# Prompt attention by pairs of heads from an earlier place, value products of two chunks side by side, and one pool of normed rows

## The chip, the cores and the metric

The kernel runs on one core of one Trainium2 chip. The time is device microseconds of one execution, and the kernel before takes 842.46 us (median of 3 runs, 838.32 to 845.08).

## What is computed

One layer of a hybrid decoder in float32, for a prompt of 512 rows and for 8 sequences of 4 new rows each (32 sample rows), which read 4096 past rows each from a paged cache. Cut to its core:

```
z = rms_norm(x, norm_mix) @ w_in                     # 1024 -> 2560 columns
q, k = rms_norm per head and half (4 heads x 2 x 64); v = z[1024:1536] (4 x 128)
u = gelu(z[1536:2048]); gv = rms_norm(gelu(z[2048:2560]))
p = softmax(mask(q k^T / 8))                         # per head and half, causal
att = (p[half 0] - lam * p[half 1]) @ v              # sample rows: over cache_k, cache_v and the new rows
mix = u * (tril(w_spatial) @ gv + b)                 # in chunks of 128 rows
h = x + [rms_norm(att) * 0.8 ; mix] @ w_out
y = h + relu(rms_norm(h) @ w_up)^2 @ w_down
```

It also returns the normed keys, the values and gv of the new rows.

## The kernel before

**Three streams share the engines.** TensorE (PE in the profile) runs the dense layers of the prompt: the input projection (`in_proj`), the output projection (`out_proj`) and eight groups of the feed-forward layer (`ffn`). Weights come in pieces of 512 KB on the SP queue and are split into two parts of reduced precision, `wh` (ScalarE, ACT) and `wl` (VectorE, DVE); the activations likewise into `Thi` and `Tlo`, and each product is three matmuls (`d<-wh,Thi`, `d<-wl,Thi`, `d<-wh,Tlo`; in `ffn` the weights are the stationary side).

**The input projection** goes through ten pieces of 256 columns in the order q0 q1 k0 k1 v0 v1 g0 g1 u0 u1 (`pi` 0 to 9), each in two halves of two row tiles (`tp`), each of these in two halves of the contraction: eight steps a piece, each ending in a `yield`. A step's follow-up work is put off by `later` and released by `flush`. Norms of q and k, and of attention rows, have a power on GpSimd (POOL, `rsqrt`).

**The prompt's attention** is a generator, `attention()`: 16 units (row tile i, head h) in the order of i. A unit is `attn_a` (scores `d<-r,r`, mask, maxima, exponentials, the two halves combined), one unit later `attn_b` (transposes `d<-idt,t`, copied out by ACT), two units later `attn_c` (product with v, `d<-r,t`). It advances once per step from step 11 of 20 on (`ATT0`, the second half of v1), two calls a unit, 36 calls in all. At that step everything put off is released at once and the pool of normed rows (`zn`) is closed and opened anew with 3 buffers in place of 8 (`local_pool(3)`), which makes room for attention's 6 tiles `t`.

**The samples' attention over the cache** is a list of small steps, `micro`: 64 chunks, each of 1 MB of keys and 1 MB of values, gathered by GpSimd's indirect DMA (`gK` into `kraw`, 2 buffers; `gV` into `v`, 3 buffers). DVE transposes a key chunk (`k_tr`, `kt<-kraw`), PE takes the scores of two chunks (`scores`, `S<-kt,qz`, 16 matmuls on 32 columns of the array each), and `LAG` = 11 chunk steps later the product with the values (`av`, `O<-v,PT`, 4 matmuls on 32 columns). `gV(n + 3)` is issued behind `av(n)` and waits for it, since it refills that chunk's buffer; `gK(n + 2)` behind `k_tr(n)`. `ptr` copies the transposed probabilities `PT` with 16 copies on ACT. With every `yield` the driver hands the step's cost to `pump`, which takes as many small steps as that cost pays for; so the cost that `attention()` yields moves the cache stream forward as well. A chunk step costs 6.1 units (TAU times 1.0), 0.6 of that before chunk 11 and 0.4 of it behind chunk 64, when no keys are left.

Each engine works through its own queue in order; within a window of 28 instructions on PE and DVE a scheduler decides that order when the kernel is built.

Of the kernel before, what the change touches and what calls it, by code (L numbers as in the profile page):

```python
# [19 lines left out]
NCH = 64  # L20
# [11 lines left out]
PLX = 2  # L32
WINDOW = 28
P_AT = 10
ATT0 = 11
ATTW = 2.4
D0 = 0.6
D1 = 0.4
# [24 lines left out]
def kernel(  # L63
# [76 lines left out]
    def st_():  # L140
        return sm.tile([128, 24], F32, tag="s", name="s")
# [46 lines left out]
    cst = const.tile([128, 13], F32, name="cst")  # L188
    rst = cst[:, 8:13]
    mhalf = const.tile([128, 24], F32, name="mhalf")  # L190
    rst8 = const.tile([128, 4], F32, name="rst8")
    ssb = [const.tile([128, 24], F32, name=f"ssb{i}") for i in range(2)]
    neglam = const.tile([128, 1], F32, name="neglam")
# [14 lines left out]
    ml = smp.tile([64, 32], F32, name="ml")  # L208

    WL = []  # L210
    for c0 in (0, 256, 512, 768, 1024, 1280, 2048, 2304, 1536, 1792):
        for hf in range(2):
            WL.append((wi[:, 4 * hf:4 * hf + 4, c0:c0 + 256], True))

# [446 lines left out]
    for n in range(NCH + LAG + 2):  # L661
        a, c = [], []
        if 1 <= n <= VB:
            a.append((gV, (n - 1,)))
        if n >= 2 and n % 2 == 0 and n <= NCH:
            a.append((scores, (n // 2 - 1,)))
            if n % 8 == 0:
                a.append((sm1, (n // 8 - 1,)))
        m = n - LAG
        if 0 <= m < NCH:  # L670
            a.append((av, (m,)))
            if m % 8 == 7:
                a.append((fin1, (m // 8,)))
        if m > 0 and m % 8 == 0:
            (a if m == NCH else c).append((fin2, (m // 8 - 1,)))
        for k, part, at, slot in ((0, 0, P_AT, a), (0, 1, P_AT, a), (1, 0, P_AT + 1, c), (1, 1, P_AT + 2, c)):
            if n >= at and (n - at) % 8 == 0 and (n - at) // 8 < 8:
                slot.append((ptr, ((n - at) // 8, k, part)))
        if 2 <= n < NCH:
            (a if n % 2 else c).append((k_tr, (n,)))  # L680
        if n >= 9 and (n - 1) % 8 == 0 and n - 1 <= NCH:
            a.append((sm2, (n // 8 - 1,)))
        d = D0 if n < LAG else D1 if n >= NCH else 1.0
        micro.append((d / 2, a))
        micro.append((d / 2, c))
# [134 lines left out]
    def in_proj(gm, F, gsrc, junk):  # L820
# [36 lines left out]
        att = attention()  # L857
        nt = new_tokens()
        for pi in range(10):
            kind, p = "qkvgu"[pi // 2], pi % 2  # L860
            if pi == 4:
                aux["vs"] = vgs
            if pi == 6:
                R3 = big.tile([128, 4 * T], F32, tag="r3", name="mix")
                R.append(R3)
                mix.append(R3[:, 0:2048].rearrange("p (n c) -> p n c", n=4))
                aux["gvs"] = vgs
            ss = ssb[pi % 2]
            items = []
            if kind == "q":  # L870
                A_, B_ = held[p]
            else:
                A_, B_ = w_get(), w_get()
            for tp in range(2):
                pss = {}
                if 2 * pi + tp == ATT0:
                    for _ in range(4):
                        flush()
                    local_pool(3)
                for half, w in ((0, A_), (1, B_)):  # L880
                    for t in (2 * tp, 2 * tp + 1):
                        cost = next(att, 0.0) if 2 * pi + tp >= ATT0 else 0.0
                        if half == 0:
                            pss[t] = dt_()[:, 0:256]
                        optB(pss[t], t, *w, half)
                        if t == 3 and (half == 0 or pi != 1):
                            w_conv()
                        if t % 2 == 1:
                            flush()
                        if half == 1:  # L890
                            post(kind, p, t, pss[t], 128, ss, items)
                            if pi == 4 and t == 0:
                                params()
                            if pi == 4 and t == 3:
                                params2()
                            if pi == 9 and t > 0:
                                cat_tile(t - 1)
                            if t == 3 and items:
                                finish_piece(kind, p, ss, items)
                            if pi == 0 and t == 1:  # L900
                                pinned(False)
                        elif pi == 5:
                            next(nt, None)
                        if pi == 0:
                            if t == 1 and half == 0:
                                x_stat(1, xt[1:4], 128, junk, G)
                                x_tile(3)
                            if t == 1 and half == 1:
                                masks(F, gsrc)
                            if t == 3 and half == 0:  # L910
                                gcols(gsrc)
                        if pi == 1 and t == 0 and half == 1:
                            load_params()
                        yield 1.3 + cost
                    if tp == 0 and kind != "q":
                        if half == 0:
                            sps = dt_()[0:64, 0:256]
                        packed(*w, [(4 * half + b, b) for b in range(4)], sps, half == 0, half == 1)
                        if half == 1:
                            post(kind, p, 4, combine(sps)[0:32], 32, ss, items)  # L920
                        yield 0.9
# [79 lines left out]

    def attn_c(i, h):
        at = aux.pop(("at", i, h))
        if h == 0:
            aux["oss"] = st_()
        ss = aux["oss"]
        o = dt_()[:, 0:128]
        for s in range(i + 1):
            mm(o, at[:, 128 * s:128 * s + 128], vN[:, s, 128 * h:128 * h + 128], s == 0, s == i)
        cat = qT[:, :, 128 * i:128 * i + 128]  # L1010
        a = aux.pop(("l", i, h))
        A.activation(out=cat[:, h, :], in_=o, func=ACTF.Copy, scale=a[:, 4:5])
        A.activation(out=o, in_=o, func=ACTF.Square, scale=a[:, 4:5], accum_out=ss[:, h:h + 1])
        if h == 3:
            rsqrt(ss[:, 0:4], EPS, 1.0 / 128.0)

            def go():
                for j in range(4):
                    V.scalar_tensor_tensor(out=cat[:, j, :], in0=cat[:, j, :], scalar=ss[:, j:j + 1], in1=sg,
                                           op0=ALU.mult, op1=ALU.mult)  # L1020
            later(go)
# [9 lines left out]
            split(ps.rearrange("p (k t) -> p k t", k=4), k0, i)  # L1031

    def attention():
        units = [(i, h) for i in range(4) for h in range(4)]
        n = len(units)
        for s in range(n + 2):
            cost = 0.0
# [8 lines left out]
            if 0 <= s - 2 < n:  # L1046
                attn_c(*units[s - 2])
                cost += 0.21 * (units[s - 2][0] + 1)
            yield ATTW * cost

    def out_proj(att):
        acc.extend(R[2 + m // 4][:, (m % 4) * T:(m % 4) * T + T] for m in range(8))
# [351 lines left out]
```

## Time and profile before

| | |
|---|---|
| runs | 842.46 us median (838.32 to 845.08) |
| the profiled execution | 842.67 us, of which the span of its instructions is 841.0 us |
| PE busy | 812.3 us (97% of the span) |
| DVE, ACT, POOL busy | 547.7, 357.9, 187.0 us |
| moved by DMA | 219.06 MB, mean 260 GB/s |

The stages in the span: 0 to about 42 us start and the samples' q; to about 300 us the input projection, with the prompt's attention (scores `d<-r,r`) from 130.1 to 260.9 us; to about 356 us the output projection; then the feed-forward groups. The cache stream runs from 42 to 582 us. A busy PE is not one at its peak, because ends of matmuls are modelled; what a piece of work costs PE is read from the start of one instruction to the start of the next.

### The profile page before, as it was taken

The page shows a single profiled execution, that of the slowest core. Times are in us where ns is not written, and L with a number is a line of the kernel's source. Part 1 is how long each engine was busy: PE and PEld are TensorE (multiplying, and loading weights), DVE is VectorE, ACT ScalarE, POOL GpSimd, SP SyncE. Part 2 cuts the span into 40 slices and gives each one's busy share as a digit, 9 for nine tenths or more (in the row PEclk, how much of TensorE's full clock was granted, in tenths as well). Part 3 has the DMA queues.
Part 4 walks back from the last instruction along what each step waited for, and adds up shares of the span by engine and source line. Part 5 has one row for each costly group of instructions (what it writes and reads, how often), then busy time and mean ns, then how long its engine had stood idle before and what let it go on. Part 6 is the DMA issues. An engine that isn't in the chain of part 4 may idle for free.

```text
span 841.0 us, 15425 instructions
## 1 busy us (share of the span) xinstructions
PE 812.3 (97%) x6210; PEld 630.6 (75%) x6210; DVE 547.7 (65%) x957; ACT 357.9 (43%) x888; POOL 187.0 (22%) x196
## 2 busy tenths in 40 slices
PE   5899999999899999999999999999999999999997
PEld 5788788676566788876666766655776898998997
DVE  5978766899888954787767576633844535444354
ACT  4543734776564652735144144163332431331231
POOL 4453532243432321212222232120100000000000
PEclk8899999999999999999999999999999999999999
DMA  8496799788788889877989797786398177577302
GB/s 316 156 376 227 264 356 317 298 317 328 279 312 322 296 307 334 291 244 281 321 316 344 294 346 275 281 294 230 116 317 267 61 237 245 177 234 232 101 14 94
DMA packets 101796, 219.06 MB, mean 260 GB/s; under 512 B 6088, under 2 KB 83996, under 8 KB 85340
## 3 DMA queue, kind: packets, MB, share of 16 engines
q0 software_dynamic: 18432, 134.23, 42.7%
q1 hardware_dynamic: 83292, 83.84, 30.5%
q8 instruction: 49, 0.80, 0.4%
q14 instruction: 23, 0.19, 0.1%
HBM read 213.53 MB, written 4.52 MB: 259 GB/s over the span
## 4 chain that ended last, share of the span: by engine, by line
PE 77%; DVE 8%; ACT 7%; DMA 5%; issue 2%; POOL 1%; SPq 0%; DVEq 0%; POOLq 0%; ACTq 0%
PE d L52 66%; PE O L52 6%; PE S L52 5%; DVE kt L52 3%; ACT PT L52 3%; DMA kraw<-in_cache_k_dram,idxK 2%; DMA raw<-in_w_in_dram 2%; DVE wl L52 1%; ACT wh L52 1%; DMA sg<-in_subln_gain_dram 1%; ACT z L52 1%; DVE s L52 1%; ACT t L52 1%; DVE zn L52 1%; ACT P L52 0%
## 5 line engine op out<-in xcount | busy, mean ns | idle before, releaser
L52 ACT CAST wh<-raw 128x1024 fp32r<-128x1024 f32 x90 | 94.1, 1047 | 189.2 <-PE d L52 175.4
L52 PE MATMUL d<-a,wh 128*128 128x272 f32 (+1 forms) x704 | 168.2, 342 | 0.4 <-DVE a L52 0.4
L52 DVE STREAM_TRANSPOSE kt<-kraw 128x2048 f32<-128x2048 f32 x64 | 146.8, 2300 | 13.5 <-PE S L52 7.1
L52 DVE TENSOR_TENSOR wl<-raw,wh 128x1024 fp32r<-128x1024 f32 x90 | 109.3, 1218 | 54.6 <-ACT wh L52 54.2
L52 PEld LDWEIGHTS d<-a,wh 128*128 128x128 f32 x704 | 112.8, 188 | 29.4 <-issue 7.1
L52 POOL DMA_INDIRECT v<-in_cache_v_dram,idxK x64 | 72.9, 1139 | 269.8 <-PE O L52 252.2
L52 PE MATMUL d<-wh,Thi 128*128 128x256 f32 x432 | 127.6, 296 | 0.6 <-ACT d L52 0.5
L52 PE MATMUL d<-wl,Thi 128*128 128x256 f32 x432 | 122.4, 283 | 0.0
L52 PE MATMUL d<-wh,Tlo 128*128 128x256 f32 x432 | 122.1, 283 | 0.2 <-DVE Tlo L52 0.2
L52 PE MATMUL d<-Thi,wh 128*128 128x272 f32 (+2 forms) x368 | 109.8, 339 | 0.0
L52 PE MATMUL d<-Tlo,wh 128*128 128x272 f32 (+2 forms) x368 | 106.7, 330 | 1.9 <-DVE Tlo L52 1.9
L52 PE MATMUL d<-Thi,wl 128*128 128x272 f32 (+2 forms) x368 | 106.8, 330 | 0.0
L52 PE MATMUL d<-a,wl 128*128 128x272 f32 (+1 forms) x352 | 102.7, 336 | 0.0
L52 PEld LDWEIGHTS d<-wh,Thi 128*128 128x128 f32 x432 | 81.6, 189 | 17.1 <-issue 11.5
L52 POOL DMA_INDIRECT kraw<-in_cache_k_dram,idxK x64 | 69.1, 1080 | 104.5 <-DVE kt L52 59.8
L52 PEld LDWEIGHTS d<-wh,Tlo 128*128 128x128 f32 x432 | 81.6, 189 | 0.9 <-issue 0.4
L52 PEld LDWEIGHTS d<-Thi,wh 128*128 128x128 f32 x368 | 63.7, 189 | 24.5 <-issue 15.0
L52 PEld LDWEIGHTS d<-wl,Thi 128*128 128x128 f32 x432 | 81.4, 188 | 0.0
L52 PE MATMUL O<-v,PT 128*32 128x512 f32 x512 | 73.4, 607 | 1.2 <-ACT PT L52 1.2
L52 ACT COPY PT<-d 32x128 f32<-32x128 f32 x256 | 65.6, 256 | 14.4 <-DVE d L52 11.0
L52 PEld LDWEIGHTS d<-Tlo,wh 128*128 128x128 f32 x368 | 63.9, 189 | 8.5 <-DVE Tlo L52 2.2
L52 PEld LDWEIGHTS d<-Thi,wl 128*128 128x128 f32 x368 | 63.7, 189 | 6.1
(265 smaller groups left out, 1069.3 us busy)
## 6 DMA issues: line engine op xcount, KB each, us to landing
raw<-in_w_up_dram SPq DMA_DIRECT2D x32, 512.0 KB, 5.3
raw<-in_w_down_dram SPq DMA_DIRECT2D x32, 512.0 KB, 3.9
plain<-in_w_up_dram SPq DMA_DIRECT2D x20, 512.0 KB, 4.3
plain<-in_w_down_dram SPq DMA_DIRECT2D x20, 512.0 KB, 6.0
raw<-in_w_in_dram SPq DMA_DIRECT2D x18, 512.0 KB, 8.2
raw<-in_w_out_dram SPq DMA_DIRECT2D x8, 512.0 KB, 6.6
plain<-in_w_out_dram SPq DMA_DIRECT2D x8, 512.0 KB, 8.7
r<-in_x_prompt_dram SPq DMA_DIRECT2D x4, 512.0 KB, 8.3
```

The lines of the kernel that those rows point to most:

```text
L52: r = f(*args, **kw)
```

## The change

1. **Attention by pairs of heads, from piece 4 on.** The units go heads 0 and 1 over all four row tiles, then heads 2 and 3. The pieces' order becomes q0 q1 k0 v0 k1 v1 g0 g1 u0 u1, so that the keys and values of heads 0 and 1 are there after four pieces, and `attention()` starts at piece 4 (`ATT0 = 4` now counts pieces). In the first eight units it yields once more, at cost 0: three calls a unit, 44 calls in all. The preparation of parameters (`params`) follows v0 to piece 3, the new rows' attention moves to piece 6. The sums of squares of the attention rows of all tiles stand in one tile `oss`.
2. **Value products by two.** `av` of an even chunk is held until its odd neighbour's step; both, and both `gV`, go together.
3. **One pool of normed rows.** `zn` keeps 8 buffers; the release of all put-off work at step 11 is gone. Room comes from the scratch for GpSimd's DMA descriptors, now 8192 bytes of each partition (16384 by default).

```diff
-ATT0 = 11
+ATT0 = 4
...
+    oss = const.tile([128, 16], F32, name="oss")
...
-    for c0 in (0, 256, 512, 768, 1024, 1280, 2048, 2304, 1536, 1792):
+    for c0 in (0, 256, 512, 1024, 768, 1280, 2048, 2304, 1536, 1792):
...
-        if 0 <= m < NCH:
+        if 0 <= m < NCH and m % 2:
+            a.append((av, (m - 1,)))
             a.append((av, (m,)))
...
-            kind, p = "qkvgu"[pi // 2], pi % 2
-            if pi == 4:
+            kind, p = ("q0", "q1", "k0", "v0", "k1", "v1", "g0", "g1", "u0", "u1")[pi]
+            p = int(p)
+            if pi == 3:
...
-                if 2 * pi + tp == ATT0:
-                    for _ in range(4):
-                        flush()
-                    local_pool(3)
...
-                        cost = next(att, 0.0) if 2 * pi + tp >= ATT0 else 0.0
+                        cost = next(att, 0.0) if pi >= ATT0 else 0.0
...
-                        elif pi == 5:
+                        if pi == 6 and tp == 0:
                             next(nt, None)
...
-        if h == 0:
-            aux["oss"] = st_()
-        ss = aux["oss"]
+        ss = oss[:, 4 * i:4 * i + 4]
...
-        units = [(i, h) for i in range(4) for h in range(4)]
+        units = [(i, 2 * hp + h) for hp in range(2) for i in range(4) for h in range(2)]
...
             yield ATTW * cost
+            if s < n // 2:
+                yield 0.0
...
-    nc = _bacc.Bacc("TRN2", target_bir_lowering=False, num_devices=1)
+    nc = _bacc.Bacc("TRN2", target_bir_lowering=False, num_devices=1,
+                     dynamic_dma_scratch_size=8192)
```

What the change does to the order of instructions shows best at three places. The first is PE in the middle of the feed-forward layer, where a value chunk's four products are `O<-v,PT 32x512 x4`, between the dense layer's matmuls. Before:

```order
L52 MATMUL d<-Thi,wl 128x512
L52 MATMUL S<-kt,qz 32x256 x16
L52 MATMUL O<-v,PT 32x512 x4
L52 MATMUL d<-Thi,wh 128x512
L52 MATMUL d<-Tlo,wh 128x512
```

Of the change, at the same scores:

```order
L52 MATMUL d<-Thi,wl 128x512
L52 MATMUL S<-kt,qz 32x256 x16
L52 MATMUL O<-v,PT 32x512 x8
L52 MATMUL d<-Thi,wh 128x512
L52 MATMUL d<-Tlo,wh 128x512
```

Before, one chunk stands right behind the scores and the next one alone, 24 dense matmuls later; now both stand behind the scores. Over the whole program PE leaves its dense matmuls for `S` or `O` 78 times in the order of before and 52 times in that of the change; the numbers of matmuls of each kind are the same.

The second place is POOL's queue in the input projection, from the norm of an attention row tile (`s`, now `oss`) on. Before:

```order
L52 DMA kraw<-in_cache_k_dram,idxK 128x2048
L52 TENSOR_SCALAR s<-s 128x4
L52 TENSOR_TENSOR s<-s,mhalf 128x4
L52 DMA v<-in_cache_v_dram,idxK 128x2048
L52 TENSOR_SCALAR ssb_118<-ssb_118 128x10
```

Of the change:

```order
L52 DMA v<-in_cache_v_dram,idxK 128x2048 x2
L52 TENSOR_SCALAR oss<-oss 128x4
L52 TENSOR_TENSOR oss<-oss,mhalf 128x4
L52 DMA kraw<-in_cache_k_dram,idxK 128x2048 x2
L52 TENSOR_SCALAR ssb_120<-ssb_120 128x10
```

Gathers of values and keys took turns; now two of values stand before two of keys, and norms (`ssb`, `oss`) stand behind either.

The third is PE at the end of the cache stream, chunks 62 and 63, with the dense layer's down projection (`d<-a,wh`) behind them. Before:

```order
L52 MATMUL d<-Tlo,wh 128x512
L52 MATMUL d<-Thi,wl 128x512
L52 MATMUL O<-v,PT 32x512 x8
L52 MATMUL d<-a_4390,wh 128x512 x2
L52 MATMUL d<-a_4390,wl 128x512
```

Of the change:

```order
L52 MATMUL d<-Thi,wl 128x512
L52 MATMUL O<-v,PT 32x512 x4
L52 MATMUL d<-a_4383,wh 128x512 x2
L52 MATMUL d<-a_4383,wl 128x512
L52 MATMUL O<-v,PT 32x512 x4
L52 MATMUL d<-a_4383,wh 128x512 x2
```

Before, chunks 56 to 61 stand 12 dense matmuls apart, each alone; now the pairs 56 and 57, 58 and 59, 60 and 61 stand 24 apart, and only 12 lie between chunk 61 and chunk 62. Chunks 54 and 55 have three dense matmuls between them, as 62 and 63 have; 12 and one tiny matmul stand between chunk 53 and chunk 54.

## Rows read from the trace of the kernel before

**Rows 1.** The page: busy time of each engine with its share of the span and its instructions, then the span in 40 slices (tenths busy; the clock that TensorE was granted, in tenths).

```profile
PE 812.3 (97%) x6210; PEld 630.6 (75%) x6210; DVE 547.7 (65%) x957; ACT 357.9 (43%) x888; POOL 187.0 (22%) x196
...
PE   5899999999899999999999999999999999999997
...
DVE  5978766899888954787767576633844535444354
...
PEclk8899999999999999999999999999999999999999
```

**Rows 2.** The waits of PE alone, from 140 to 300 us (engine, tile, what it waited for; us in total, times, the longest).

```profile
PE d L52 <- ACT t L52: 2.2, 2, 1.8
PE d L52 <- issue: 1.7, 1, 1.7
PE S L52 <- DVE qz L52: 1.5, 1, 1.5
PE d L52 <- ACT PT L52: 0.6, 1, 0.6
PE d L52 <- ACT d L52: 0.5, 1, 0.5
```

**Rows 3.** The timeline of PE around one value chunk that stands alone (start us, us, instruction, shapes).

```profile
564.07 0.40 PE L52 MATMUL d<-Thi,wl 128*128 128x512 f32 x1
564.40 1.06 PE L52 MATMUL O<-v,PT 128*32 128x512 f32 x8
565.40 0.50 PE L52 MATMUL d<-Thi,wh 128*128 128x512 f32 x1
...
565.97 0.39 PE L52 MATMUL d<-Thi,wl 128*128 128x512 f32 x1
566.20 0.39 PE L52 MATMUL d<-Thi,wh 128*128 128x512 f32 x1
```

**Rows 4.** The same timeline around the scores of two chunks with one value chunk behind them.

```profile
542.86 0.40 PE L52 MATMUL d<-a,wl 128*128 128x512 f32 x1
543.19 1.93 PE L52 MATMUL S<-kt,qz 128*32 128x256 f32 x32
544.94 1.04 PE L52 MATMUL O<-v,PT 128*32 128x512 f32 x8
545.91 0.50 PE L52 MATMUL d<-Thi,wh 128*128 128x512 f32 x1
```

**Rows 5.** The same timeline around scores with no value chunk behind them, in the input projection.

```profile
52.09 0.28 PE L52 MATMUL d<-wq,Tlo 128*128 128x256 f32 x1
52.30 1.93 PE L52 MATMUL S<-kt,qz 128*32 128x256 f32 x32
54.16 0.39 PE L52 MATMUL d<-wh,Thi 128*128 128x256 f32 x1
54.39 0.28 PE L52 MATMUL d<-wl,Thi 128*128 128x256 f32 x1
```

**Rows 6.** The same timeline at the two last value chunks, and one line on what the tile O waited for.

```profile
579.97 0.40 PE L52 MATMUL d<-Thi,wl 128*128 128x512 f32 x1
580.29 2.11 PE L52 MATMUL O<-v,PT 128*32 128x512 f32 x16
582.33 0.73 PE L52 MATMUL d<-a,wh 128*128 128x512 f32 x2
...
  DMA v<-in_cache_v_dram,idxK: 0.9, 1
```

**Rows 7.** The same timeline at the longest stop of PE behind 300 us that the change reaches, where chunk 56 waits for its probabilities.

```profile
557.02 1.06 PE L52 MATMUL O<-v,PT 128*32 128x512 f32 x8 [1.16 <-ACT PT L52]
```

**Rows 8.** POOL's timeline at the end of the cache stream, then, for the tile v from 540 to 583 us, the time from issue to landing.

```profile
561.81 0.94 POOL L52 DMA_INDIRECT v<-in_cache_v_dram,idxK  x1 [2.48 <-PE O L52]
565.77 0.94 POOL L52 DMA_INDIRECT v<-in_cache_v_dram,idxK  x1 [3.02 <-PE O L52]
...
DMA to landing us min/median/max: 5.7/7.4/8.3
```

**Rows 9.** The stretches of the input projection from 105 us on: us, then busy us and instructions of PE, PEld, DVE, ACT and POOL, the granted clock, the DMA engines' mean busy share, GB/s.

```profile
105.00:126.00 21.00, 21.00 (x204) 17.00 (x196) 14.34 (x36) 7.53 (x19) 7.56 (x6) 1.00 0.99 357
126.00:147.00 21.00, 21.00 (x195) 17.21 (x192) 14.11 (x29) 8.46 (x26) 4.68 (x5) 1.00 0.94 318
147.00:168.00 21.00, 19.08 (x166) 13.78 (x165) 17.98 (x45) 15.33 (x52) 5.90 (x6) 1.00 0.81 299
168.00:189.00 21.00, 20.95 (x169) 14.90 (x172) 19.27 (x51) 15.73 (x54) 10.37 (x10) 1.00 0.87 315
189.00:210.00 21.00, 20.35 (x189) 13.39 (x190) 19.74 (x41) 13.35 (x39) 7.35 (x7) 1.00 0.87 327
...
273.00:294.00 21.00, 20.44 (x186) 15.75 (x188) 19.54 (x42) 14.17 (x42) 7.26 (x7) 1.00 0.85 290
```

**Rows 10.** Key gathers: what their tile kraw shows from 147 to 300 us, and then the same line from 45 to 63 us, where up to four gathers are under way at once.

```profile
DMA to landing us min/median/max: 5.5/7.8/10.3
...
DMA to landing us min/median/max: 8.5/9.3/12.7
```

**Rows 11.** PE's timeline from 157 to 262 us, two of the scores in the densest stretch.

```profile
188.93 1.94 PE L52 MATMUL S<-kt,qz 128*32 128x256 f32 x32
200.14 1.93 PE L52 MATMUL S<-kt,qz 128*32 128x256 f32 x32
```

More of the change, by code (lines that the diff above doesn't have):

```diff
@@ L891, in in_proj @@
                             post(kind, p, t, pss[t], 128, ss, items)
-                            if pi == 4 and t == 0:
+                            if pi == 3 and t == 0:
                                 params()
-                            if pi == 4 and t == 3:
+                            if pi == 3 and t == 3:
                                 params2()
```

## The prediction, as it was written before the result

> **What bounds the kernel now.** I read the page first. PE is busy for 97% of the span and DVE for 65%; PE drops out of the highest tenth in the first slices and in a few places behind them, and its clock is granted nearly in full from the third slice on [rows 1]. So time can be won in two ways only: PE gets less to do, or one of its stops goes. The start (to 42 us) and everything behind 582 us keep their instructions. Next I read PE's own waits in the stretch of the prompt's attention: five kinds, 2.2 + 1.7 + 1.5 + 0.6 + 0.5 = 6.5 us in all, with ACT, DVE and one unexplained "issue" as causes [rows 2]. The stretches say why: from 147 to 210 us, and again from 273 to 294, DVE is busy for 18 to 19.7 of 21 us, and ACT for 13 to 16, while from 105 to 147 us they are at 14 and 8 [rows 9]. Last I read, from start to start, what a change to the narrow products costs PE.
>
> **The pairs on PE.** Where a value chunk stands alone, the start of the next dense matmul is 1.33 us behind that of the last one; less the 0.23 us that one dense matmul takes anyway, the chunk costs 1.10 us [rows 3]. Scores with one chunk behind them cost 3.05 - 0.23 = 2.82 us [rows 4], scores alone 2.07 - 0.12 = 1.95 us [rows 5]. So a chunk behind other narrow products costs 0.87 us, and 0.23 us of a lone chunk is the way there and back. The order goes there 78 times before and 52 times now: 26 x 0.23 = 6.0 us less. The other end comes from the one place where two chunks stand together: 2.36 - 0.23 = 2.13 us, the second at 1.03, only 0.07 below a lone one [rows 6]. By that the gain is 1.8 us. But the same group shows that this second chunk waited for its gather, so I take 6.0.
>
> **The end of the cache stream.** A value gather starts 0.31 us behind the product that frees its buffer (the product of rows 3 ends at 565.46, the gather of rows 8 starts at 565.77) and lands 5.7, 7.4 or 8.3 us later (least, median, most) [rows 8]: 7.7 us behind the product at the median. Before, a chunk's gather was freed by the product three chunks earlier. In a pair, the second chunk (say 2k+3) is freed by the first product of the pair ahead (2k), so only 2k+1, the dense matmuls between the pairs and 2k+2 lie between. Where the stream still has keys, a pair comes round in 11.2 us at the densest [rows 11], and that is enough. Behind the keys' end it is not. Between two pairs 24 matmuls apart lie 0.87 + 24 x 0.23 + 0.23 + 0.87 = 7.5 us: chunks 59 and 61 wait 0.2 us each. Chunk 55 has chunk 53, 12 dense matmuls, chunk 54 and three matmuls ahead of it: 0.87 + 2.8 + 1.10 + 0.7 + 0.23 and the tiny one, 5.8 us: it waits 1.9. Chunk 63 likewise has 5.7 us and waits 2.0. Sum 4.3 us; with the least landing time 0.5, with the most 8.3. PE works in order, so every dense matmul behind such a product waits too. Two stops of before go off: the 0.16 us by which the last pair is now above 2 x 0.87 + 0.23 [rows 6], and 1.16 us in which chunk 56 waits for ACT's copies [rows 7], since that chunk now comes a chunk step later. Net: 4.3 - 0.2 - 1.2 = +2.9 us (from -0.9 to +6.9).
>
> The Trainium skill ("DMA: Bandwidth & Descriptors", on the anatomy of a DMA of the software path) gives such a gather about 2.0 us plus its bytes at 436 GB/s, an estimate of 4.4 us for 1 MB. By it no chunk would wait at the end and the sum below would be 4.3 us lower, at 833. The trace disagrees: beside the other traffic even the least landing time is 5.7 us [rows 8].
>
> **Attention from piece 4.** The same matmuls run, on PE nothing is saved as such; what can go are the 6.5 us of stops [rows 2]. Half of the units (heads 0 and 1) move into k1, v1 and g0, the first two of which lie where DVE has some 6.7 us free of each 21 and ACT 13 [rows 9], and each unit there has three calls for its chain of maxima, exponentials and copies, not two. The other half stays beside g1 and u, and attention ends half a piece ahead of the output projection. The bounds are 0 and 6.5 us. DVE is not emptied in the later pieces, only thinned, and the key transposes, the weights' split and the chain of `gelu` stay, so I take half: 3.2 us less.
>
> Against that stands a price. Attention's cost also drives the cache stream, so k1 and v1 now get more gathers, besides the outputs of k and v. In these stretches the DMA engines are already at 0.99 and 0.94 of their time with 357 and 318 GB/s [rows 9], while PE shows no idle time there at all. If DMA holds the stream back a little, PE waits for a chunk it had in time before. The bounds are nothing, and what the key rival below gives. I take +1 us, one short wait.
>
> **Edits at no cost.** The pool of 8 normed rows, `oss` and the earlier `params` add no instruction to an engine; the earlier `params` hides behind a PE that is busy there, and what it loads was requested two pieces earlier. If that load were late, k0's and v0's follow-up would stall for one landing, which the ranges below hold. The released work at step 11 went through queues that PE did not wait for [rows 9]. The scratch for descriptors is halved: four gathers at once were under way from 45 to 63 us [rows 10] with the whole of it. If the half held only two, the third of a group would be issued late, and that is again the key rival.
>
> **The sum.** 842.67 (the profiled execution, 841.0 of it span) - 6.0 - 3.2 + 2.9 + 1.0 = 837.4 us, so I say 837. The median of the runs is 842.46, practically the same, so the change would be -0.6%.
>
> **Rivals.**
> - *The stops go, and the gathers land early.* DVE has been the cause of most stops and loses a third of attention in the dense pieces. Then -6.0 - 6.5 - 0.9: 829 us. For it: no stop of PE in 105 to 147 us [rows 9]. Against it: ACT's 16 copies of `PT` come in one go whenever they come.
> - *Keys late (slower).* POOL now issues value, value, key, key. Both value gathers wait for PE's product, and the first key gather stands behind them. Counted from the start of the scores: 1.75 us scores, two products, so POOL is free for the key at about 5 us, with two gathers ahead of it in line. If it lands 7.8 us later, as the median is with one ahead [rows 10], it is there at 12.8 us; the next pair needs it at 11.2 + 1.9 = 13.1 us in the densest place [rows 11]. So it decides from a landing time of 8 us on. At 10.3 us, the most between 147 and 300 us [rows 10], DVE would stand still for 2.2 us in each of some eight pairs, 18 us, of which DVE has about 1.5 us to spare in each 21 us [rows 9], 8 us over the stretch; the rest reaches PE, +10 us: 847 to 848, and with 12.7 us, the most of the crowded stretch [rows 10], it is beyond 851. For it: three gathers in a row landed at 8.5 to 12.7 us there. Against: a key has a second buffer, and PE needs a pair of keys only at the next scores. The norms' powers stand in the same queue, behind gathers that wait for PE.
> - *It does not do what it says.* A second chunk costs 1.03 us, as in the only place shown, and the stops only change places: 842.67 - 1.8 + 2.9 = 844 us.
>
> **How the numbers follow.** Forecast 0.45, stops gone 0.25, keys late 0.15, no gain 0.15. The forecast's own range is 832 to 842 (half of the stops either way, and most of the end's bounds). For 8 in 10 I reach to the first rival's 829, a little below it for a gain at its end, and up over the third's 844 and the second's 848: 828 to 848. About 1% is what a measurement can tell from no change, 834 to 851 around the median. Below 834 lie nearly all of the first rival and a small part of the forecast: 0.31. Above 851 lies the worse half of the second and a little for what I have not seen: 0.11. The rest is 0.58.
>
> **What would show it.** Each step has its row in the profile of the changed kernel. The timeline of PE should show `S x32` and `O x16` in one go, 3.7 us from the last dense start to the next (1.95 + 2 x 0.87). If the second chunk costs 1.0, the first term is wrong. The waits of PE should show `O <- DMA v` with about 4 us, all between 540 and 590 us; any such wait earlier, or DVE `kt <- DMA kraw` beyond 105 us (there is none now), speaks for late keys or values. PE's waits of the stretch up to 300 us should come to about 3 us; if they stay at 6 us with other names, spreading attention only moved them. Scores `d<-r,r` should start near 95 us, not 130, and the stretches from 147 us on should show DVE below 18 of 21 us. Wrong altogether would be a stop of several us for POOL's powers (`ssb`, `oss`) or a landing time of values beyond 9 us in the whole stream.

## The result: 852 us, slower by 1.3%, and the profile after

The changed kernel takes 852.12 us (median of 4 runs, 849.22 to 858.21), the kernel before 842.24 us beside it (4 runs). The ratio is 1.0132 with a 95% interval of 1.0100 to 1.0163. The prediction said 837 us, with 848 as the upper end. Ratios come with the measurement and are not the quotients of the medians. Two of the runs below, `e4_p2_later` and `g_rows_55`, had one execution each in a slower state of the chip, which their medians here leave out.

The profiled execution of the changed kernel took 849.22 us with a span of 847.5, 6.5 us more than the span before. It was the fastest of the four, so the profile shows 6.5 of the 9.9 us by which the medians differ. These lines of its page answer to [rows 1] (busy time, share, instructions; the span in 40 slices; the granted clock):

```profile
PE 809.8 (96%) x6210; PEld 637.5 (75%) x6210; DVE 545.6 (64%) x957; ACT 357.7 (42%) x888; POOL 181.7 (21%) x196
...
PE   5999899999799999989999999998999999999997
...
PEclk8799999999899999999999999999999999999999
```

PE is busy for 2.5 us less than before, and idle for 847.5 - 809.8 = 37.7 us, where it was 841.0 - 812.3 = 28.7. So PE did less and stood 9.0 us longer; that is the whole difference. The eleventh slice (212 to 233 us) stands out: PE at 7 tenths, its clock at 8. Its waits from 140 to 300 us answer to [rows 2]:

```profile
PE S L52 <- DVE kt L52: 4.2, 1, 4.2
PE d L52 <- ACT PT L52: 1.4, 2, 1.0
PE d L52 <- ACT t L52: 1.4, 2, 1.2
PE d L52 <- ACT z L52: 0.7, 2, 0.6
PE d L52 <- DVE zn L52: 0.5, 1, 0.5
```

They come to 4.2 + 1.4 + 1.4 + 0.7 + 0.5 = 8.2 us, where they were 6.5 before and the prediction looked for about 3. A further stop of 2.6 us stands before 140 us, and new ones stand behind 300 us. The timeline of PE at the largest new stops (in brackets the idle time before the instruction and what ended it):

```profile
99.83 0.21 PE L52 MATMUL d<-z,Em 128*32 128x20 f32 x2 [2.57 <-DVE z L52]
...
229.54 1.08 PE L52 MATMUL S<-kt,qz 128*32 128x256 f32 x8 [4.17 <-DVE kt L52]
...
350.67 0.33 PE L52 MATMUL d<-idt,h 128*128 128x128 f32 x1 [1.50 <-DVE h L52]
...
427.40 0.39 PE L52 MATMUL d<-s,Rm 128*128 128x4 f32 x2 [1.97 <-DVE s L52]
```

The waits of PE from 300 to 600 us show the end of the stream as well:

```profile
PE O L52 <- DMA v<-in_cache_v_dram,idxK: 3.5, 3, 1.5
PE d L52 <- DVE s L52: 2.5, 2, 2.0
PE d L52 <- DVE h L52: 1.5, 1, 1.5
PE d L52 <- DVE Tlo L52: 1.4, 1, 1.4
PE d L52 <- DVE z L52: 0.7, 1, 0.7
```

By stages, PE's idle time goes from 12.0 to 11.3 us up to 42 us, from 1.5 to 3.7 us up to 140, from 6.8 to 8.2 us up to 300, and from 3.5 to 9.6 us behind it up to the end of the stream. So 6.0 of the 9.0 us lie behind 300 us, in the waits just shown.

What stood ahead of the key transpose that PE waited for at 229.5 us is read from DVE's timeline:

```profile
218.82 2.30 DVE L52 STREAM_TRANSPOSE kt<-kraw 128x2048 f32<-128x2048 f32 x1
...
223.68 1.23 DVE L52 TENSOR_TENSOR wl<-raw,wh 128x1024 fp32r<-128x1024 f32 x1 [1.20 <-ACT wh L52]
224.82 1.14 DVE L52 SCALAR_TENSOR_TENSOR r<-r,oss,sg 128x128 f32<-128x128 f32 x4
...
227.18 2.30 DVE L52 STREAM_TRANSPOSE kt<-kraw 128x2048 f32<-128x2048 f32 x1
```

No one of these is new. Between the two transposes lie a unit's chain, a weight split that waits 1.2 us for ACT, and the rescaling of a row tile of attention; the scores are next in PE's order, and it stands for 4.17 us.

The clock adds to it. The same stretches as in [rows 9] (columns as there), then two pieces of the trace cut at the edges of the granted clock:

```profile
84.00:105.00 21.00, 18.28 (x151) 15.92 (x150) 17.04 (x51) 15.74 (x52) 8.18 (x6) 0.93 0.75 261
105.00:126.00 21.00, 21.00 (x208) 15.72 (x207) 13.60 (x24) 8.24 (x26) 5.50 (x6) 0.99 0.73 263
...
147.00:168.00 21.00, 20.66 (x191) 14.57 (x192) 16.13 (x34) 15.18 (x49) 3.74 (x4) 1.00 0.98 394
168.00:189.00 21.00, 21.00 (x176) 13.47 (x171) 15.51 (x23) 13.36 (x41) 5.85 (x6) 1.00 0.70 237
...
210.00:231.00 21.00, 15.78 (x117) 8.90 (x115) 19.07 (x53) 15.80 (x52) 5.86 (x7) 0.93 0.79 289
231.00:252.00 21.00, 20.80 (x181) 14.81 (x180) 15.78 (x36) 11.46 (x39) 7.70 (x9) 0.90 0.68 243
```

```profile
102.00:105.40 3.40, 3.40 (x18) 3.40 (x17) 1.21 (x6) 3.26 (x14) 0.00 (x0) 0.50 1.05 390
...
228.20:235.10 6.90, 5.56 (x29) 4.75 (x30) 5.36 (x15) 3.73 (x16) 3.49 (x3) 0.51 0.74 271
```

Behind the stop at 97 us the clock was granted at 0.50, the lower level of 1.2 GHz, for 3.4 us, and behind the stop at 225 us for 6.9 us. What that costs is read from the starts of two dense matmuls of 256 columns ahead of the first stretch and of two within it:

```profile
96.27 0.28 PE L52 MATMUL d<-wl,Thi 128*128 128x256 f32 x1
96.39 0.27 PE L52 MATMUL d<-wh,Tlo 128*128 128x256 f32 x1
...
103.13 0.41 PE L52 MATMUL d<-wl,Thi 128*128 128x256 f32 x1
103.34 0.41 PE L52 MATMUL d<-wh,Tlo 128*128 128x256 f32 x1
```

Over 14 of them the mean is 0.119 us from start to start, and 0.213 us over 15 in the stretch, so at the full level the same work takes 0.56 of the time. PE was busy in the two stretches for 3.40 + 5.56 us, so they cost about 4.0 us. Before, the clock was at full in all of [rows 9], and behind the start one stretch of the kind stood at 364.5 us:

```profile
364.50:367.90 3.40, 3.40 (x16) 1.51 (x15) 2.75 (x7) 0.00 (x0) 1.44 (x2) 0.50 0.86 292
```

It cost 1.5 us, by the same reckoning; the start, up to 42 us, has a mean granted clock of 0.84 in either profile. The account of the two profiles is then: +9.0 for idle time and +2.5 for the clock (4.0 - 1.5); of the 6.5 us seen, that leaves -5.0 for PE's work itself, where the prediction had -6.0. The Trainium skill ("TensorE: Matmul & The Clock Gate", on HAM oscillation) tells of a kernel that waits for transfers between tiles and starts each at the lower clock again; these rows show the same behind single waits for DVE.

### The profile page after: what moved, and what is told of

Same layout as the page of the kernel before. It is cut to its first block, busy times and chain, and to the rows that moved or that the text cites. A ratio compares the mean times of both kernels' runs of the same rounds, so it can differ in the third digit from the quotient of the medians.

```text
span 847.5 us, 15414 instructions
## 1 busy us (share of the span) xinstructions
PE 809.8 (96%) x6210; PEld 637.5 (75%) x6210; DVE 545.6 (64%) x957; ACT 357.7 (42%) x888; POOL 181.7 (21%) x196
## 4 chain that ended last, share of the span: by engine, by line
PE 57%; DVE 13%; DMA 12%; issue 9%; ACT 6%; POOL 2%; SPq 0%; DVEq 0%; POOLq 0%; ACTq 0%
PE d L52 51%; DVE kt L52 6%; PE S L52 3%; PE O L52 3%; DMA v<-in_cache_v_dram,idxK 3%; DMA raw<-in_w_in_dram 2%; DMA raw<-in_w_up_dram 2%; DMA raw<-in_w_down_dram 2%; DVE wl L52 2%; ACT wh L52 2%; DMA z<-in_x_prompt_dram 1%; DVE s L52 1%; ACT z L52 1%; ACT PT L52 1%; DMA kraw<-in_cache_k_dram,idxK 1%
## 5 line engine op out<-in xcount | busy, mean ns | idle before, releaser
L52 DVE STREAM_TRANSPOSE kt<-kraw 128x2048 f32<-128x2048 f32 x64 | 146.5, 2299 | 13.6 <-PE S L52 11.6
L52 PE MATMUL d<-wh,Thi 128*128 128x256 f32 x432 | 129.3, 299 | 0.9 <-ACT z L52 0.6
L52 PE MATMUL d<-wl,Thi 128*128 128x256 f32 x432 | 124.6, 289 | 0.0
L52 PE MATMUL d<-wh,Tlo 128*128 128x256 f32 x432 | 123.9, 287 | 0.0
L52 POOL DMA_INDIRECT v<-in_cache_v_dram,idxK x64 | 66.4, 1037 | 265.0 <-PE O L52 256.2
L52 POOL DMA_INDIRECT kraw<-in_cache_k_dram,idxK x64 | 71.3, 1114 | 106.3 <-DVE kt L52 63.1
L52 PEld LDWEIGHTS d<-wh,Thi 128*128 128x128 f32 x432 | 83.7, 194 | 10.5 <-issue 6.8
L52 PEld LDWEIGHTS d<-wh,Tlo 128*128 128x128 f32 x432 | 83.7, 194 | 0.7 <-issue 0.4
L52 PEld LDWEIGHTS d<-wl,Thi 128*128 128x128 f32 x432 | 83.6, 193 | 0.0
L52 PE MATMUL O<-v,PT 128*32 128x512 f32 x512 | 68.7, 594 | 3.5 <-DMA v<-in_cache_v_dram,idxK 3.5
L52 PE MATMUL S<-kt,qz 128*32 128x256 f32 x1024 | 66.6, 385 | 4.3 <-DVE kt L52 4.2
```

The lines of the kernel that those rows point to most:

```text
L52: r = f(*args, **kw)
```

## The experiments

First three theories stood against each other. **A**: the moved attention makes the stops. **B**: the pairs make them, since keys and values are then asked for in pairs and two key transposes stand in a row on DVE. **C**: the halved scratch holds gathers back. Ratios are to runs of the kernel before on the same chip, which had medians of 841.2 to 842.4 us.

### The parts of the change alone

Pairs alone (`e1_pairs_only`, in the kernel before):

```diff
-        if 0 <= m < NCH:
+        if 0 <= m < NCH and m % 2:
+            a.append((av, (m - 1,)))
```

> The kernel before with one edit: the products of two value chunks together. Theory A (the moved attention makes the stops): PE's waits up to 300 us stay those of before, 26 trips go (-6.0 us), the end of the cache stream costs +3: 839 us, -3 against before. Theory B (the pairs make the stops: keys and values are asked for in pairs, two key transposes stand in a row on DVE): stops of 1.4 to 2 us for DVE behind 340 us show up as in the changed kernel, with the value waits at the end they eat the 6 us: 842 to 845 us. Theory C (the halved scratch) expects 836 to 839 here, since the scratch is whole.

The change without the pairs (`e2_no_pairs`, those lines taken back):

> The changed kernel with single value chunks again, all else as changed. Theory A: the stops at 97, 145 and 225 us and the half clock behind two of them stay, the trips come back (+6.0), the value waits at the end (3.5) and the two stops for key transposes in a row (3.4) go: 851 us, still 8 to 9 above before. Theory B: without the pairs the stops are those of before: 842 to 845 us. Theory C: slower than before, by late gathers: kraw and v landing medians over 9 and 8 us between 105 and 300 us stay.

The scratch alone (`e5_half_scratch`, `dynamic_dma_scratch_size=8192` in the kernel before):

> The kernel before with one edit: the scratch for descriptors halved to 8192 bytes. Theory C (less scratch holds the gathers back): landing medians between 105 and 300 us rise from 7.9 (kraw) and 6.8 (v) toward the changed kernel's 9.4 and 8.0, POOL's gathers issue later, and the time rises by 3 us or more: 845 or above. Theories A and B: nothing changes, 842 us, within 1.

`params2` later in the change (`e4_p2_later`):

```diff
-                            if pi == 3 and t == 3:
+                            if pi == 6 and t == 3:
                                 params2()
```

> The changed kernel, but params2 (which stands at the end of v0 and makes PE wait 2.6 us at 97 us for a DVE copy behind two key transposes) runs three pieces later, at the end of g0. If that stop and the half clock behind it (3.4 us at 1.2 GHz) are worth what the ledger of the two profiles gives, 852 - 2.6 - 1.7 = 848 us. If the wait for DVE only moves to the next instruction that needs it (theory B or C, where DVE is late anyway), 851 to 852 us.

| run | median us | ratio | interval |
|---|---|---|---|
| e1_pairs_only | 842.82 | 1.0016 | 0.9991 to 1.0042 |
| e2_no_pairs | 852.35 | 1.0125 | 1.0108 to 1.0142 |
| e5_half_scratch | 841.05 | 0.9992 | 0.9978 to 1.0006 |
| e4_p2_later | 852.68 | 1.0166 | 1.0127 to 1.0205 |

C falls: the scratch does nothing. The whole loss is there without the pairs, so A holds so far. Without the pairs the profile has a span of 851.4 and PE busy for 817.2 us, so 34.2 idle: 5.5 more idle than before, and 4.9 us more busy with the same matmuls. Behind the start it has stretches at the lower clock behind four stops, where the kernel before had the one at 364.5 us, but fewer of them in the start: the mean granted clock of the whole span is 0.990 against 0.989. So the clock does not explain the 4.9 us by itself, and their cause was not separated. Its idle time is 11.6 us from 140 to 300 us and 4.4 behind that: of the 9.6 us that the changed kernel stands behind 300 us, most comes with the pairs. The pairs alone gain nothing: their PE is busy for 807.6 us of 841.6, 4.7 less than before, and idle for 5.3 more. Of that, 3.2 us are waits for values at the end (3 times). So B is right for the pairs' own gain, though not for the loss.

Moving `params2` away removed the stop at 97 us and gained nothing. The same instruction of PE stopped longer in its new place, behind two key transposes and a weight split on DVE:

```profile
190.51 0.21 PE L52 MATMUL d<-z,Em 128*32 128x20 f32 x2 [4.87 <-DVE z L52]
```

### Early start, density, and a buffer for the pairs

The change without pairs and with attention's old starting place (`e6_late_start`); the change without pairs and without the empty third call (`e8_two_calls`):

```diff
-ATT0 = 4
+ATT0 = 11
...
-                        cost = next(att, 0.0) if pi >= ATT0 else 0.0
+                        cost = next(att, 0.0) if 2 * pi + tp >= ATT0 else 0.0
```

```diff
-            if s < n // 2:
-                yield 0.0
```

(`e6_late_start` has the second edit too.)

> The changed kernel with single value chunks, and attention starts where it did before (second half of v1's place, 36 calls, no empty third call); the new order of pieces, the units by pairs of heads, the earlier params and the pool of 8 normed rows stay. Theory A1 (the early start beside k1, v1 and g0 makes the stops, since gathers, norms and the attention's chains then share DVE and ACT): the time is that of before, 841 to 843 us. Theory A2 (the new order of the pieces, or the order of the units, makes them, wherever attention starts): it stays at 850 to 853 us.

> The changed kernel with single value chunks, without the empty third call: attention starts early as in the change and runs at the density of before, so that it ends about one and a half pieces ahead of the output projection. Theory A1 (the early start as such): stops as without this edit, 850 to 853 us. Theory A3 (what hurts is that it lasts longer, beside more of the other chains): 845 to 848 us. If denser is worse, 855 or more.

Two versions of the kernel before with pairs: a fourth value buffer in the room that the scratch leaves (`e7_pairs_vb4`), and single chunks at the end (`e9_pairs_not_end`):

```diff
-VB = 3
+VB = 4
```

```diff
+        if 0 <= m < NCH and (m % 2 or m >= 52):
+            if m < 52:
+                a.append((av, (m - 1,)))
             a.append((av, (m,)))
```

> The kernel before with value chunks in pairs, a fourth value buffer and the halved scratch that makes room for it. Pairs alone gave 842.8 us, with 3.2 us of PE's waits for value gathers at the end of the stream. If the missing buffer is what eats the pairs' gain, these waits go to less than 0.5 us and the time falls to 838 to 839. If the pairs' gain is lost to DVE (two key transposes in a row) and to the clock behind stops between 150 and 350 us, at most 1 us goes: 841 to 843.

> The kernel before with value chunks in pairs up to chunk 51 and single behind it, where no keys are left. Against pairs throughout, six trips come back (+1.4 us) and the value waits of the end go (-3.2 us), ACT's stop at chunk 56 may return (+1.2): 842 us if the stops before 350 us stay, 840 at the best. It tells, beside the fourth buffer, whether the end is what the pairs lose.

| run | median us | ratio | interval |
|---|---|---|---|
| e6_late_start | 852.91 | 1.0122 | 1.0099 to 1.0144 |
| e8_two_calls | 849.65 | 1.0090 | 1.0070 to 1.0111 |
| e7_pairs_vb4 | 835.86 | 0.9923 | 0.9898 to 0.9948 |
| e9_pairs_not_end | 841.21 | 0.9993 | 0.9973 to 1.0013 |

The early start is acquitted: with attention back in its old place the loss is the same (A1 falls). The empty third call costs 2.7 us (852.35 - 849.65): less than theory A3 asked for (that attention hurts by lasting longer), and hardly clear of the spread, since the two intervals just meet. And the pairs do pay: with a fourth buffer, 5.5 us faster than before, beyond what was expected. That kernel's waits of PE from 300 to 600 us show none for values; what is left is a stop of 3.7 us in the profiled run, where two key transposes stand in the middle of the softmax's short operations:

```profile
PE d L52 <- DVE s L52: 3.7, 1, 3.7
PE d L52 <- DVE Tlo L52: 1.4, 1, 1.4
PE d L52 <- DVE h L52: 1.1, 1, 1.1
```

Leaving the pairs out at the end alone won 1.6 us of the 7 that the buffer wins, with the value waits at the end gone in either. But the single chunks bring back six trips (1.4 us by the prediction's price) and ACT's stop of 1.2 us at chunk 56, so the end may be worth some 4 of the 7 us. Where the rest lies was not separated.

### Which part of the new order

The pieces' order, with the earlier `params` and the pool that go with it, and attention by rows from its old place (`e10_pieces_only`: `e6_late_start` with the old order of units); the units' order alone in the kernel before (`e11_units_only`, with the tile `oss`); the pool with the halved scratch (`e12_one_pool`); the fourth buffer with the halved scratch (`e13_vb4_single`). The diff is that of `e10_pieces_only` against `e6_late_start`:

```diff
-    units = [(i, 2 * hp + h) for hp in range(2) for i in range(4) for h in range(2)]
+    units = [(i, h) for i in range(4) for h in range(4)]
```

> The kernel before with the new order of the pieces (k0, v0, k1, v1), params and params2 one piece earlier, new_tokens in g0 and the pool of 8 normed rows with the halved scratch; attention starts and runs by rows as before, value chunks single. The late start with the units by pairs of heads gave 852.9 us, so the loss of some 11 us lies in the order of pieces, in the order of units or in the pool. If it is the pieces (stops for params2 at 98 to 103 us, for the norms of k0 at 59 us and for the keys of k1 beside v1): 850 to 853 us. If it is the units: 841 to 843. If both carry part: 845 to 849.

> The kernel before with one edit: the units of attention by pairs of heads (with the tile oss that this needs), the pieces in their old order. Two short units at each end of two ramps, and the powers and rescalings of all four rows in the second half, beside g and u. If the order of units makes the stops (as 221, 244 and 292 us in the run with the late start), 848 to 853 us; if the pieces make them, 841 to 843.

> The kernel before with one pool of 8 normed rows throughout, no release of the pending work at step 11, and the halved scratch that makes room. If the pool or the released work matters, 845 us or more (the first waits of attention at 130 to 150 us change); if it is one of the edits at no cost, 841 to 842 us.

> The kernel before with a fourth value buffer and the halved scratch, value chunks single. Pairs with this buffer gave 835.9 us against 841.4. If the pairs' 26 trips are the gain and the buffer only lets it through, this run stays at 841 to 842 us (before has no wait for a value gather to lose). If the buffer itself is the gain, 836 us.

| run | median us | ratio | interval |
|---|---|---|---|
| e10_pieces_only | 846.26 | 1.0056 | 1.0036 to 1.0075 |
| e11_units_only | 848.63 | 1.0078 | 1.0059 to 1.0098 |
| e12_one_pool | 841.24 | 1.0004 | 0.9988 to 1.0019 |
| e13_vb4_single | 840.98 | 0.9986 | 0.9971 to 1.0001 |

Both orders carry a part, 5.0 and 7.4 us, and the pool none. A buffer without pairs wins nothing, so the 5.1 us between the last run and `e7_pairs_vb4` come with the pairs. They are a net gain: in the two profiles PE is 5.9 us less busy with the pairs and 4.2 us longer idle, and the profiled execution of `e7_pairs_vb4` is the slowest of its six. The units' order has a clear face in PE's waits (84 to 312 us), and the longest of them in its timeline, with ACT's row behind it:

```profile
PE d L52 <- ACT PT L52: 6.9, 4, 2.9
PE S L52 <- DVE qz L52: 2.8, 2, 2.4
PE d L52 <- ACT t L52: 1.5, 3, 1.0
```

```profile
291.68 1.16 PE L52 MATMUL d<-r,t 128*128 128x128 f32 x8 [2.92 <-ACT PT L52]
```

```profile
287.35 4.28 ACT L52 COPY PT<-d 32x128 f32<-32x128 f32 x16 [3.27 <-DVE d L52]
```

The stream's 16 copies `PT` (4.28 us on ACT) start late, and PE stands until they are through. What the product of the unit needs of them is not shown: its own copy `t` was done at 278.6 us. By the kernel's code the copies read one of the tiles `d` that are handed out in turn, and the product writes such a tile, so it may have waited for that tile to come free. Before, the same meeting cost 0.6 us [rows 2]. That raised a doubt: is it the order of units, or where the stream happens to stand when a unit comes?

### Shifting the stream

Theory **U**: the order costs this by itself. Theory **M**: what counts is how the stream meets the rest. One number, `D0`, makes the first eleven chunk steps shorter or longer and so moves the stream against the pieces and units:

```diff
-D0 = 0.6
+D0 = 0.55
```

(0.65 in the runs that end in 65; `g_rows` is the kernel before, `g_pairs` is `e11_units_only`.)

> The kernel before with D0 = 0.55 for 0.6: the cache stream's first eleven chunk steps are shorter, so that the whole stream stands about half a step (some 3 us of PE) earlier against the pieces and the units; units by rows as before. If the units' new order costs what it costs by itself (theory U), a shifted stream moves the time by little: 840 to 843 us. If what counts is only how the stream's copies PT, its transposes and qz meet the units' chains (theory M, meeting by chance), units by rows can lose as well: 838 to 850, away from 841 by more than 3.

> The kernel before with D0 = 0.65: the stream stands about half a step later; units by rows. Theory U: 840 to 843 us. Theory M: anywhere from 838 to 850, and not near 841 in both shifted runs.

> The run with the units by pairs of heads alone (848.6 us), with D0 = 0.55. Theory U: it stays about 7 us above the rows with the same D0. Theory M: its stops (2.9 us at 288, 2.4 at 218, 1.9 at 162 us, all for PT or qz) go or change places, and the distance to the rows with the same D0 is under 3 us or has the other sign.

> The units by pairs of heads alone, with D0 = 0.65. Theory U: about 7 us above the rows with the same D0. Theory M: the distance differs from 7 us by more than 4, in this run or in the one with 0.55.

| D0 | units by rows | by pairs of heads |
|---|---|---|
| 0.55 | 854.21, ratio 1.0167 (1.0132 to 1.0203) | 849.39, 1.0089 (1.0062 to 1.0117) |
| 0.60 | the kernel before | 848.63, 1.0078 (1.0059 to 1.0098) |
| 0.65 | 848.75, 1.0074 (1.0048 to 1.0100) | 859.85, 1.0208 (1.0178 to 1.0238) |

U falls. A shift of about half a chunk step (11 x 0.05) costs the kernel before 12 and 6 us, with not one instruction added, and the price of the units' order goes from -4.8 over +7.4 to +11.1 us. The 12 us are more than theory M had allowed for. The prices of the pieces' order and of the third call are known at one place of the stream only. The waits of PE from 42 to 300 us for units by rows at 0.55, against [rows 2]:

```profile
PE d L52 <- ACT t L52: 8.2, 7, 3.0
PE S L52 <- DVE qz L52: 2.5, 1, 2.5
PE d L52 <- ACT PT L52: 1.0, 2, 0.8
PE S L52 <- DVE kt L52: 1.0, 1, 1.0
PE d L52 <- ACT d L52: 0.5, 1, 0.5
```

The waits for units' copies `t` are 8.2 us in 7, where they were 2.2 in 2. The shift is not pure: the kernel's code divides a fixed total cost among the steps (TAU), so the later steps change by 0.9% the other way and the shift fades toward the stream's end; and it also packs the first chunks closer, and the 2.5 and 1.0 us for `qz` and `kt` stand at 83 and 71 us, before any unit.

Two last runs ask the same of the changed kernel: `D0 = 0.55` in it (`h_after_55`), and a fourth value buffer, with 5 normed rows for 8 to make room (`h_after_vb4`).

> The changed kernel with D0 = 0.55 for 0.6. If the changed kernel's loss hangs on how the stream meets the units (theory M), its time moves by more than 3 us, to either side of 852: 843 to 849 or 855 to 865. If the loss lies in the orders themselves (theory U), 850 to 854.

> The changed kernel with a fourth value buffer and, to make room, 5 normed rows for 8. If the parts add up (order of pieces and units +11, pairs that have their buffer -5.5), the value waits at the end (3.5 us) go and the time is 846 to 848 us. If five rows make the norms wait, or the buffer can do nothing for a kernel with stops elsewhere, 851 to 853.

`h_after_55` took 844.13 us (1.0034, 1.0013 to 1.0055): one number takes back 8 of the 10 us, and the rest stays: it is not faster than the kernel before. The long stop is gone; of 210 to 252 us these two lines are of the changed kernel and of this run:

```profile
210.00:252.00 42.00, 36.58 (x296) 23.71 (x294) 34.86 (x88) 27.26 (x91) 13.56 (x15) 0.92 0.74 266
```

```profile
210.00:252.00 42.00, 40.31 (x336) 26.58 (x336) 39.42 (x92) 29.89 (x96) 16.13 (x17) 1.00 0.71 267
```

Its value waits at the end stayed, 4.8 us in 3, and other stops came up: over the whole span PE is idle for 38.5 us, against 37.7 in the changed kernel, and busy for 804.8 against 809.8, at the same mean granted clock of 0.985. So these profiles do not show that fewer stops took the 8 us back; where PE's work became shorter was not found. `h_after_vb4` took 858.18 us (1.0203, 1.0184 to 1.0222), where 846 to 848 was expected from adding the parts and 851 to 853 if the buffer could do nothing. Its value waits went, but the attention's stops grew: one alone is 5.5 us for a unit's copy `t`. Whether the five rows or once more the meeting is at fault was not separated.

## Why the prediction was wrong, point by point

Against the 837.4 us of the sum, the profiled execution is 11.8 us longer: 4.7 us in the stretch of attention from 140 to 300 us, 2.2 ahead of it, 3.1 behind 300 us, 2.5 for the clock and 1.0 for PE's work, less 0.7 at the start and the 1.0 that late gathers were given.

- **Pairs, -6.0 us: right in kind, and read too small.** The timeline of PE in the changed kernel, in the output projection, has the block that the prediction priced at 1.95 + 2 x 0.87 = 3.69 us:

```profile
321.09 0.27 PE L52 MATMUL d<-wh,Tlo 128*128 128x256 f32 x1
321.29 1.93 PE L52 MATMUL S<-kt,qz 128*32 128x256 f32 x32
323.04 1.90 PE L52 MATMUL O<-v,PT 128*32 128x512 f32 x16
324.87 0.38 PE L52 MATMUL d<-wh,Thi 128*128 128x256 f32 x1
325.09 0.28 PE L52 MATMUL d<-wl,Thi 128*128 128x256 f32 x1
325.21 0.28 PE L52 MATMUL d<-wh,Tlo 128*128 128x256 f32 x1
```

  From dense start to dense start that is 3.78 us, less 0.12 for the dense matmul 3.66. The lower bound (a second chunk at 1.03 us) is out. But the way back goes on behind the next dense start: that matmul takes 0.22 us to the following one and not 0.12. Before, it is the same behind the lone chunk of [rows 3], 0.33 us for 0.23, by the line that the fence there leaves out:

```profile
565.73 0.40 PE L52 MATMUL d<-Tlo,wh 128*128 128x512 f32 x1
```

  So a trip costs 0.33 us, and 26 of them 8.6. In the changed kernel the work became only 5.0 us less; what took the rest was not separated. With a fourth buffer the pairs' net gain was 5.1 us.
- **End of the stream, +2.9 us net: the value waits right in kind and sum, the other stops missing.** The value waits were 3.5 us in 3 (0.8, 1.2 and 1.5, where 1.9, 0.2, 0.2 and 2.0 were predicted), all between 550 and 590 us, and ACT's stop at chunk 56 went. With the longest landing time the prediction's own sum is 7.9 us, not 8.3. By the estimate from the Trainium skill ("DMA: Bandwidth & Descriptors", on the anatomy of a DMA of the software path) there would have been none; the measurement decides. But the new stops for DVE behind 300 us (2.5 us for `s`, 1.5 for `h`, 0.7 for `z`) had no term, and idle time there rose by 6.0 us for 2.9.
- **Half of attention's stops go, -3.2 us: this step failed.** They grew, from 6.5 to 8.2 us between 140 and 300 us, with 2.6 us at 97 us besides, and without the pairs the first were 11.4 us. Attention did spread as planned: its scores start at 100 us and not at 130, and from 147 to 189 us DVE is busy for 16.1 and 15.5 us, where it was for 18.0 and 19.3 [rows 9]. I took the stops for a matter of DVE's and ACT's load in a stretch, and load alone does not decide: in `h_after_55` DVE is busy for 39.4 us of 42 from 210 to 252 us, more than the 34.9 of the changed kernel, and PE stands for 1.7 us there and not for 5.4. In the stops that were read one by one, a queue holds a link of a unit or of the stream behind some 2 to 4 us of other work when it is next in PE's order. The bounds of nothing and 6.5 us were the worse mistake, since they left no room for new stops.
- **The price of the clock: left out.** The two long stops were followed by 10.3 us at 1.2 GHz, worth 4.0 us.
- **Edits at no cost: half right.** Pool and scratch cost nothing. The new order of pieces cost 5 us at this place of the stream, with stops of 1.3 and 0.4 us around `params2` at 100 us among its rows, and the new order of units 7.4; as losses they had no term at all.
- **Late gathers, +1.0 us: no cause.** The rival of late keys came nearest with its price, beyond 851 us, but by luck, since it was wrong as a mechanism: no wait of PE ahead of 550 us is put down to a gather. Between 147 and 300 us key gathers landed in 6.3, 8.2, 10.4 us (least, median, most), hardly above [rows 10], though from 105 to 300 us their median rose from 7.9 to 9.4 us; and there was no stop of several us for POOL's powers. Two of the prediction's signs could not tell: DVE waited for keys for 1.6 us in 2 beyond 105 us, but already before for 1.2 us in 2, where the prediction says none, and landings of values beyond 9 us were there before as well (10.9 us at most, now 10.4). And in [rows 2] ACT holds 3.3 of the 6.5 us and DVE 1.5, so DVE was not the cause of most stops.

The third rival had the stops change places, but not grow. So the rival that should have held most was not on the list: a schedule whose numbers suit one order can lose when the order changes. That the changed kernel with numbers of its own would beat the kernel before is not shown; its best time is 844.13 us.

## What to carry to other kernels

When several streams share in-order engines under fixed numbers, a reorder is a new schedule: shift one of those numbers in the kernel before first, and see how much the time moves with no work changed. Here that is 6 to 12 us, where the single edits tried moved the time by 0 to 7.4, and a change is fairly judged only after its own numbers are set. An edit that shortens PE's work should be tried alone and with the buffer that it newly needs: the pairs were worth nothing with three value buffers and 0.8% with four, the fastest version found (835.86 us).

## What the runs showed of the hardware

- PE's clock fell to 1.2 GHz behind single long stops, for 3.4 to 6.9 us, so that a stop of 4.17 us at 225 us cost about 2.5 us more than itself (5.56 us of work in the stretch, which at the full level takes 0.56 of that). Not every stop did it: the one of 1.83 us at 159 us in the kernel before had the full clock behind it [rows 9].
- Leaving the dense matmuls for the narrow products and coming back cost 0.33 us a trip here, of which 0.10 us stands behind the first dense matmul.
- Much of the spread between runs may be the clock. The profiled run of `e12_one_pool`, whose median is that of the kernel before, has a mean granted clock of 0.996 against 0.989, and a span of 836.5 us with PE busy for 808.6, against 841.0 and 812.3 before: the idle time is the same within 0.8 us, the busy time with the same matmuls is 3.7 us less. This was not tested by itself.
